# Reciprocal square roots and the causal mask's addition on VectorE in place of GpSimd, in a hybrid decoder block

## The chip, the cores and the metric

One of the cores of a Trainium2 chip runs the kernel. The core has five engines with an in-order queue each: TensorE (PE, with its weight loads shown apart as PEld), VectorE (DVE), ScalarE (ACT), GpSimd (POOL) and SyncE (SP), which here issues transfers. The metric is the device time of one execution in microseconds (us). Lower is better.

## The reference

The block works on 256 tokens of 2048 channels: a SwiGLU feed-forward of half weight, a token mixer, a second feed-forward, a gated per-layer embedding, and a last rmsnorm. The mixer has 8 gated delta-rule heads and 16 state-space heads in chunks that share one input and one output projection. Cut to what matters here:

```
def rmsnorm(x, w):
    return x * lax.rsqrt(jnp.mean(x * x, axis=-1, keepdims=True) + EPS) * w
def l2norm(x):
    return x * lax.rsqrt(jnp.sum(x * x, axis=-1, keepdims=True) + EPS)
...
    q = l2norm(q) * (GDN_HEAD_DIM ** -0.5)
    k = l2norm(k)
    ...
    decay = jnp.exp(jnp.where(causal, gc[..., :, None] - gc[..., None, :], -jnp.inf))
    ...
    t_inv = lax.linalg.triangular_solve(eye + lower, eye, left_side=True, lower=True)
    ...
    seg = jnp.exp(jnp.where(causal, acs[..., :, None] - acs[..., None, :], -jnp.inf))
    ...
    o = rmsnorm(o, norm_w) * jax.nn.silu(gate)
    ...
    proj = rmsnorm(h, mix_norm) @ w_in
    h = h + jnp.concatenate([o_gdn, o_ssm], axis=-1) @ w_out
```

## The kernel before

**The products.** Every weight matrix is streamed from HBM by SP (tile `raw`), a column tile of 128 columns at a time. Half a column tile (128x1024, 8 weight tiles of 128x128) is called a piece below: ACT rounds it to `hi` (L118), DVE makes the rest `lo` = `raw` - `hi` (L119), and PE multiplies both parts with the activations, 16 matmuls for each piece (`mm`, L128, L130, L132). ACT and DVE then bring the sum out of PSUM (L168, L169). There are 4 buffers each for `hi` and `lo` and 3 for `raw`. If DVE or ACT stands still, PE goes on with what is split already and then stands too.

**The token mixer.** It runs beside the product with `win` (52 column tiles, that is 104 pieces), as generators that `tick` advances by one step after each piece. For each of four pairs of delta-rule heads, `gdn_pair` builds the matrices `LA` (DVE, L533). SP writes their diagonal blocks to HBM (`blkl`) and reads them back in another layout (`Lb`). POOL inverts the blocks by substitution: 62 small instructions on `tb` and `Z` (L582, L584), a pair of them for each of 31 columns. SP takes the result back through HBM (`blky`, then four transfers into `Y`), and DVE transposes `Y` into `oT` (L595). Larger blocks, the chunk's state and the outputs `o` follow on PE, with DVE and ACT between (`xv` L642, `st` L635). Four `ssd_quad` generators do the state-space heads.

**What the change touches.** `rsq` (L207) is the reciprocal square root of a small tile. It is called 16 times: 8 times in `stats`, for the norms over channels, and 8 times in `gdn_pair`, for the lengths of keys and queries (`rs`, 128x8) and the norm of the outputs (`ro`, 128x4). `decay` (L490) is called 12 times, once for each pair and twice for each quad. A tile `dec` (128x512) is filled by a transfer that POOL issues (`spread`, L486), the causal mask is added to it (L492), ACT takes four exponentials of it (L494), and DVE multiplies it in `LA` (L533) or by `CB` (L747).

**The end of the projections.** The last columns of `win` give the gates `zt`. When the heads are done, ACT scales `o` by `ro` (L674), PE transposes it (`ot`, L679), ACT copies it to `oT` (L680), and DVE multiplies in the gate (L810). `osp` holds both parts of the mixer's output (`split_into`, L195 on ACT and L196 on DVE) and is what `wout` is multiplied with.

**The order.** A scheduler sorts the instructions of each engine when the program is built, by its own estimates of durations. On the chip each engine works through its list in that order, and an instruction that waits holds back all that stand behind it on its engine.

Of the kernel before, what the change touches and what calls it, by code (L numbers as in the profile page):

```python
# [10 lines left out]
F32R = mybir.dt.float32r  # L11
AF = mybir.ActivationFunctionType
# [3 lines left out]
P = 128  # L16
# [13 lines left out]
# columns of the parameter pack  # L30
# [12 lines left out]
# the inverse: diagonal blocks of BS, CG columns of one per partition, then doubled  # L43
# [4 lines left out]
# columns of the constant pack: identity, upper triangle, additive causal mask, level masks, unit columns  # L48
# [7 lines left out]
def constant_pack():  # L56
# [5 lines left out]
    # the columns of the identity that the partition holds, partition = (block, group of columns)  # L62
# [6 lines left out]
def tile_hybrid_block(ctx, tc, xT, pT, con, par, wgu1, wd1, wnar, win, wout, wgu2, wd2, wproj, wple, outT):  # L69
# [30 lines left out]
    # ---------------------------------------------------------------- helpers  # L100
# [6 lines left out]
    def load(src):  # L107
        """One transfer of the stationary tiles [P, n * 128] of one column tile."""
        raw = rawp.tile([P, 2048], F32, tag="raw", name="raw")
        nc.sync.dma_start(raw[:, :src.shape[-1]], src)  # L110
        return raw

    def split(src):
        """hi + lo = src exactly, each of them wide enough for one pass."""
# [7 lines left out]
    def chain(ps, hi, lo, act_in, ks, first=True, last=True):  # L122
        """ps[:, 0] (+)= (hi + lo) @ high part, ps[:, 1] (+)= hi @ low part of act_in, for the tiles w of
        hi + lo and the tiles k of act_in."""
# [10 lines left out]
    def single(src, act_in, ks):  # L135
        """The product as a whole in ps[:, 0]."""
# [14 lines left out]
    def product(srcs, act_in, ks, out):  # L151
        """out = the product of the column tile that lies in the transfers srcs, rows ks, with act_in."""
# [18 lines left out]
    # work that runs beside the products: each generator is advanced by one step after each piece  # L171
# [14 lines left out]
    def split_x(k, wname):  # L186
        """The parts of xs are those of h * w, for one k tile."""
# [5 lines left out]
    def split_into(dst, src):  # L193
        """dst[:, :, 0] + dst[:, :, 1] = src exactly."""
        act.copy(dst[:, :, 0, :], src)  # L195
        dve.tensor_tensor(out=dst[:, :, 1, :], in0=src, in1=dst[:, :, 0, :].bitcast(F32), op=ALU.subtract)  # L196

    def sumsq(acc, src, first):
        """acc[P, 2, T] += src^2, src a pair of tiles."""
# [7 lines left out]
    def rsq(m, n, name):  # L207
        """1/sqrt(m) for a [P, n] tile."""
        y = small.tile([P, n], F32, tag=f"rsq{n}", name=name)
        pool.tensor_tensor(out=y, in0=m, in1=mhalf[:, :n], op=ALU.pow)  # L210
        t = small.tile([P, n], F32, tag=f"rsqt{n}", name=name + "t")
        dve.tensor_tensor(out=t, in0=y, in1=y, op=ALU.mult)
        dve.scalar_tensor_tensor(out=t, in0=t, scalar=-0.5, in1=m, op0=ALU.mult, op1=ALU.mult)
        dve.scalar_tensor_tensor(out=y, in0=t, scalar=1.5, in1=y, op0=ALU.add, op1=ALU.mult)
        return y

    mhalf = cp.tile([P, 16], F32, name="mhalf")
    pool.memset(mhalf, -0.5)

    def stats(squares, width, name, use, wait=2):  # L220
        """use(row): 1/sqrt(mean over width channels + eps) per token, as a row on every partition (in PSUM).
        squares: [P, T] tiles whose sum over partitions and tiles is the sum of squares."""
# [29 lines left out]
    # ---------------------------------------------------------------- loads  # L252
    warm = small.tile([P, 1], F32, tag="warm", name="warm", bufs=1)
    act.activation(warm, ones[:, 0:1], AF.Silu)
    # the array's clock rises with use: multiply while the first transfers are on their way
# [5 lines left out]
    # the first transfers alternate between the tokens and the first three column tiles  # L261
# [28 lines left out]
    # ---------------------------------------------------------------- feed-forward  # L290
    def ffn(wgu, wd, squares, next_name, start=None):
        """h += 0.5 * swiglu(rmsnorm(h)); squares: gives those of h; returns those of the new h."""
# [50 lines left out]
    # ---------------------------------------------------------------- token mixer  # L343
    with ExitStack() as mix:
# [5 lines left out]
        # halved conv weights and bias: silu(2u) = u * (1 + tanh(u))  # L350
# [13 lines left out]
        # a pair of projected tiles, behind three columns of zeros  # L364
# [8 lines left out]
        # ---- per-token scalars: a (8), dt (16), b (8) -> decay logs, dt, beta  # L373
        raw = load(wnar)
        ps = mm_bank("nar")
        for k in range(0, KD, 8):
            # both parts as columns of one stationary tile: rows 0-31 and 32-63 of the product
# [30 lines left out]
        def scalars():  # L408
# [9 lines left out]
            # log(1 + e) = 2 atanh(e / (2 + e))  # L418
# [24 lines left out]
            # the cumulated logs as rows, in DRAM to be spread over the partitions from there  # L443
# [10 lines left out]
        # ---- projection of a pair of column tiles, causal conv, silu  # L454
# [18 lines left out]
        def silu_gate(w0):  # L473
            """Twice the silu."""
# [8 lines left out]
        def spread(src):  # L483
            """Rows of gc_i on every partition."""
# [5 lines left out]
        def decay(d, c):  # L490
            """exp(gc_i - gc_j) for j <= i, else 0, as [j, n, i]; d: rows of gc_i, c: columns of -gc_j."""
            pool.tensor_tensor(out=d, in0=d, in1=over(cmask, 4), op=ALU.add)  # L492
# [3 lines left out]
        # scratch for the diagonal blocks and their inverses  # L496
        blocks = [[tc.dram_tile([4 * (P // BS), BS, BS], F32, name=f"blk{n}{i}") for n in "ly"] for i in range(2)]

        # ---- gated delta rule, two heads at a time; matrices in the order (chunk, head)
        def gdn_pair(i, KQ, V):  # L500
# [12 lines left out]
            # squares of k (the diagonal of k k^T) and of q by token  # L513
# [36 lines left out]
            # diagonal blocks of I + L inverted by substitution, CG columns of one per partition  # L550
# [11 lines left out]
            # values and (first chunk) keys by token  # L562
# [375 lines left out]
def _rows(v):  # L938
    """[n * 128] -> [128, n]."""
    return v.reshape(-1, P).T  # L940
# [61 lines left out]
```

## Time and profile before

| | |
|---|---|
| device time, median of 3 runs | 2117.88 us (2116.24 to 2119.15) |
| span of the profiled execution, first to last instruction | 2115.8 us |
| PE busy | 2064.8 us, 98% of the span |
| DVE busy | 1351.4 us, 64% |
| ACT busy | 1047.7 us, 50% |
| POOL busy | 256.7 us, 12% |

The profiled execution has no time of its own beside its span; the runs' median is 2.1 us above that span. The first feed-forward ends near 760 us of the span, the projections of the mixer near 1162 us, and the rest is the output projection, the second feed-forward, the embedding and the last norm. POOL's share is an average over a program in which it does little outside the mixer. In a list of waits the engine on the left stood idle until the engine on the right ended the instruction that is named.

### The profile page before, as it was taken

Reading aid. Unit: us, or ns where it says so; the run is one execution under the profiler, and the core shown is the slowest. Engines: PE = TensorE matmul, PEld = TensorE weight load, DVE = VectorE, ACT = ScalarE, POOL = GpSimd, SP = SyncE. Lnnn points to the kernel's source line nnn. Section 1 sums busy time; section 2 is a strip of 40 time slices with the busy share of each in tenths; the row PEclk is TensorE's granted clock in tenths of the full one; section 3 lists DMA queues with packets and bytes.
Section 4 is the critical chain, followed back from the end, with each engine's and each line's share of the span. In section 5 each row is a group of like instructions: output and inputs, shape, how many; then the busy total and the mean of one; then the engine's idle time right before and its main releaser. Section 6 shows DMA issues by size and latency. Waiting matters only on the chain.

```text
span 2115.8 us, 29521 instructions
## 1 busy us (share of the span) xinstructions
PE 2064.8 (98%) x11824; PEld 1795.9 (85%) x11824; DVE 1351.4 (64%) x1908; ACT 1047.7 (50%) x1591; POOL 256.7 (12%) x368
## 2 busy tenths in 40 slices
PE   9999999999999999888989999999999999999997
PEld 7888888888888888777878888888888888888886
DVE  7655555656556677767777666665555556556685
ACT  6444444444445555444455556544444444445554
POOL 2000000000000011667540011000000000000011
PEclk9999999999999999998999999999999999999998
DMA  7555455555545555434544555555456555545652
GB/s 261 187 182 195 158 190 184 207 191 188 182 172 179 190 198 164 163 123 148 168 137 151 194 179 187 191 189 190 163 183 211 185 193 180 190 160 190 201 194 101
DMA packets 67129, 380.77 MB, mean 180 GB/s; under 512 B 11744, under 2 KB 13024, under 8 KB 33840
## 3 DMA queue, kind: packets, MB, share of 16 engines
q1 hardware_dynamic: 65664, 374.93, 52.3%
q0 software_dynamic: 1328, 3.97, 1.0%
q8 instruction: 92, 1.51, 0.3%
q14 instruction: 45, 0.37, 0.1%
HBM read 376.21 MB, written 2.65 MB: 179 GB/s over the span
## 4 chain that ended last, share of the span: by engine, by line
PE 85%; POOL 7%; DMA 3%; issue 2%; DVE 2%; SPq 0%; ACT 0%; POOLq 0%; DVEq 0%; ACTq 0%
PE mm L130 55%; PE mm L128 26%; POOL Z L584 3%; POOL tb L582 3%; PE mm L132 2%; DMA Lb<-blkl 1%; DMA blkl<-LA 1%; DMA er<-rows 1%; DVE lo L119 1%; DMA Y<-blky 0%; PE pj L130 0%; DMA hT<-in_xT 0%; DVE LA L533 0%; POOL dec L486 0%; POOL dec L492 0%
## 5 line engine op out<-in xcount | busy, mean ns | idle before, releaser
L130 PE MATMUL mm<-xs,hi 128*128 128x512 f32 x3888 | 1367.0, 399 | 1.8 <-ACT hi L118 1.8
L119 DVE TENSOR_TENSOR lo<-raw,hi 128x1024 fp32r<-128x1024 f32 (+1 forms) x774 | 864.2, 1124 | 489.8 <-ACT hi L118 489.4
L128 PE MATMUL mm<-xs,lo 128*128 128x256 f32 x3645 | 1028.8, 282 | 6.4 <-DVE lo L119 6.4
L118 ACT CAST hi<-raw 128x1024 fp32r<-128x1024 f32 (+1 forms) x774 | 745.7, 964 | 517.7 <-PE mm L130 403.5
L130 PEld LDWEIGHTS mm<-xs,hi 128*128 128x128 f32 x3888 | 718.5, 189 | 155.9 <-ACT hi L118 2.3
L128 PEld LDWEIGHTS mm<-xs,lo 128*128 128x128 f32 x3645 | 687.5, 189 | 20.8 <-DVE lo L119 8.4
L130 PE MATMUL mm<-hid,hi 128*128 128x512 f32 x1408 | 492.5, 397 | 0.0
L128 PE MATMUL mm<-hid,lo 128*128 128x256 f32 x1344 | 377.8, 281 | 0.0
L130 PEld LDWEIGHTS mm<-hid,hi 128*128 128x128 f32 x1408 | 260.2, 188 | 59.0
L205 POOL TENSOR_TENSOR acc<-acc,sq 128x512 f32<-128x512 f32 x43 | 65.6, 1525 | 1602.3 <-ACT sq L204 1578.0
L128 PEld LDWEIGHTS mm<-hid,lo 128*128 128x128 f32 x1344 | 253.3, 188 | 3.0
L168 ACT COPY t<-mm 128x256 f32<-128x256 f32 x167 | 62.4, 374 | 158.5 <-PE mm L130 157.6
L169 DVE TENSOR_TENSOR t<-t,mm 128x256 f32<-128x256 f32 x167 | 69.9, 419 | 85.7 <-ACT t L168 85.4
L168 ACT COPY s<-mm 128x256 f32<-128x256 f32 x88 | 32.8, 373 | 148.2 <-PE mm L130 148.1
L130 PE MATMUL mm<-osp,hi 128*128 128x512 f32 x256 | 88.9, 396 | 0.0
L169 DVE TENSOR_TENSOR s<-s,mm 128x256 f32<-128x256 f32 x88 | 37.1, 421 | 73.7 <-ACT s L168 73.6
L132 PE MATMUL mm<-xs,lo 128*128 128x256 f32 x243 | 69.6, 286 | 11.7 <-DVE lo L119 11.7
L584 POOL TENSOR_TENSOR Z<-Z,tb 128x124 f32<-128x124 f32 (+30 forms) x124 | 67.8, 547 | 9.4
L128 PE MATMUL mm<-osp,lo 128*128 128x256 f32 x240 | 67.1, 281 | 0.0
L132 PEld LDWEIGHTS mm<-xs,lo 128*128 128x128 f32 x243 | 45.9, 189 | 24.5 <-DVE lo L119 14.1
L582 POOL TENSOR_TENSOR tb<-Lb,Z 128x124 f32<-128x124 f32 (+30 forms) x124 | 61.7, 498 | 27.0 <-DMA Lb<-blkl 17.9
L130 PEld LDWEIGHTS mm<-osp,hi 128*128 128x128 f32 x256 | 46.9, 188 | 10.1
(296 smaller groups left out, 1091.4 us busy)
## 6 DMA issues: line engine op xcount, KB each, us to landing
raw<-in_wgu SPq DMA_DIRECT2D x173, 1024.0 KB, 4.8
raw<-in_wd SPq DMA_DIRECT2D x128, 704.0 KB, 4.1
raw<-in_win SPq DMA_DIRECT2D x52, 1024.0 KB, 5.0
raw<-in_wout SPq DMA_DIRECT2D x16, 1024.0 KB, 4.9
raw<-in_wple SPq DMA_DIRECT2D x16, 1024.0 KB, 4.8
first<-in_wgu SPq DMA_DIRECT2D x12, 256.0 KB, 7.2
dec<-rows POOLq DMA_DIRECT2D x12, 256.0 KB, 4.7
Lb<-blkl SPq DMA_DIRECT2D x4, 512.0 KB, 5.2
```

Of the source, the lines that this page charges most:

```text
L118: act.copy(hi, src)
L119: dve.tensor_tensor(out=lo, in0=src, in1=hi.bitcast(F32), op=ALU.subtract)
L128: pe.matmul(ps[:, 0, :], lo[:, w, :], act_in[:, k, 0, :], start=False, stop=False, skip_group_check=True)
L130: pe.matmul(ps, hi[:, w, :], act_in[:, k], start=start, stop=stop, skip_group_check=True)
L132: pe.matmul(ps[:, 0, :], lo[:, w, :], act_in[:, k, 0, :], start=False, stop=False, skip_group_check=True)
L168: act.copy(out, ps[:, 0, :])
L169: dve.tensor_tensor(out=out, in0=out, in1=ps[:, 1, :], op=ALU.add)
L205: pool.tensor_tensor(out=acc, in0=acc, in1=sq, op=ALU.add)
L582: pool.tensor_tensor(out=t, in0=over(Lb[:, j, j + 1:], CG), in1=Z[:, :, j:j + 1].to_broadcast([P, CG, n]), op=ALU.mult)
L584: pool.tensor_tensor(out=Z[:, :, j + 1:], in0=Z[:, :, j + 1:], in1=t, op=ALU.subtract)
```

## The change

`rsq` no longer calls `pow` on POOL. DVE makes a first guess from the bits of the number (a shift, then a multiplication and an addition) and improves it by three Newton steps of three instructions, where one step of three followed `pow` before. The tile `mhalf` and its memset go. In `decay` the addition of the mask moves from POOL to DVE. All else in the diff is comments and docstrings.

```
+I32 = mybir.dt.int32
...
     def rsq(m, n, name):
         """1/sqrt(m) for a [P, n] tile."""
         y = small.tile([P, n], F32, tag=f"rsq{n}", name=name)
-        pool.tensor_tensor(out=y, in0=m, in1=mhalf[:, :n], op=ALU.pow)
         t = small.tile([P, n], F32, tag=f"rsqt{n}", name=name + "t")
-        dve.tensor_tensor(out=t, in0=y, in1=y, op=ALU.mult)
-        dve.scalar_tensor_tensor(out=t, in0=t, scalar=-0.5, in1=m, op0=ALU.mult, op1=ALU.mult)
-        dve.scalar_tensor_tensor(out=y, in0=t, scalar=1.5, in1=y, op0=ALU.add, op1=ALU.mult)
+        dve.tensor_scalar(t.bitcast(I32), m.bitcast(I32), 1, None, op0=ALU.logical_shift_right)
+        dve.tensor_scalar(y.bitcast(I32), t.bitcast(I32), -1.0, float(0x5F3759DF), op0=ALU.mult, op1=ALU.add)
+        for _ in range(3):
+            dve.tensor_tensor(out=t, in0=y, in1=y, op=ALU.mult)
+            dve.scalar_tensor_tensor(out=t, in0=t, scalar=-0.5, in1=m, op0=ALU.mult, op1=ALU.mult)
+            dve.scalar_tensor_tensor(out=y, in0=t, scalar=1.5, in1=y, op0=ALU.add, op1=ALU.mult)
         return y
-    mhalf = cp.tile([P, 16], F32, name="mhalf")
-    pool.memset(mhalf, -0.5)
...
         def decay(d, c):
-            pool.tensor_tensor(out=d, in0=d, in1=over(cmask, 4), op=ALU.add)
+            dve.tensor_tensor(out=d, in0=d, in1=over(cmask, 4), op=ALU.add)
```

The scheduler sorts the changed program anew. In what follows most helper lines of the changed program stand one line further down than before (L120 for L119, L131 for L130, L169 for L168, L197 for L196); the lines of `rsq` are L212, L213 (the guess) and L215 to L217 (a Newton step), and lines from L232 on have the same numbers.

On POOL, in the substitution of pair 2 (the third), the program before has this in the middle of the 62 steps, between the columns of 60 and of 48: the transfers of two `dec` tiles (those of pair 3 and of the first half of quad 1), their two additions, and two transfers for `er`.

```order
L582 TENSOR_TENSOR tb<-Lb,Z 128x60
L486 DMA dec<-rows 128x2x256
L486 DMA dec<-rows 128x512
L584 TENSOR_TENSOR Z<-Z,tb 128x4x15
L582 TENSOR_TENSOR tb<-Lb,Z 128x56
L584 TENSOR_TENSOR Z<-Z,tb 128x4x14
L492 TENSOR_TENSOR dec<-dec,cont 128x512
L582 TENSOR_TENSOR tb<-Lb,Z 128x52
L727 DMA er<-rows 64x2x128 x2
L492 TENSOR_TENSOR dec<-dec,cont 128x512
L584 TENSOR_TENSOR Z<-Z,tb 128x4x13
```

In the changed program the same transfers stand behind the last step of that substitution:

```order
L582 TENSOR_TENSOR tb<-Lb,Z 128x4
L584 TENSOR_TENSOR Z<-Z,tb 128x4
L486 DMA dec<-rows 128x2x256
L486 DMA dec<-rows 128x512
L560 COPY Z<-cont 128x128
L727 DMA er<-rows 64x2x128 x2
L590 MEMSET Y 128x512
L486 DMA dec<-rows 128x512
L582 TENSOR_TENSOR tb<-Lb,Z 128x124
```

So the two `dec` tiles are asked for some 30 steps later, and their additions, now on DVE, stand in DVE's list three pieces further on than the place at which DVE waited for them before. In pair 3 the transfers that stood in the middle (for quad 2) move likewise, to two or three steps before its end.

On PE, at the end of the projections, the program before transposes the outputs of the last pair (`ot`) among the last pieces of the product with `win` (`mm<-xs`), 66 matmuls ahead of its end:

```order
L130 MATMUL mm<-xs,hi 128x512
L679 MATMUL ot<-cont,o 128x128
L128 MATMUL mm<-xs,lo 128x256
L679 MATMUL ot<-cont,o 128x128
L130 MATMUL mm<-xs,hi 128x512
L679 MATMUL ot<-cont,o 128x128 x2
L130 MATMUL mm<-xs,hi 128x512
L132 MATMUL mm<-xs,lo 128x256
```

In the changed program they stand behind the last matmul of that product, right ahead of the first one of the output projection (`mm<-osp`):

```order
L129 MATMUL mm<-xs,lo 128x256
L131 MATMUL mm<-xs,hi 128x512
L679 MATMUL ot<-cont,o 128x128 x4
L131 MATMUL mm<-osp,hi 128x512
L133 MATMUL mm<-osp,lo 128x256
L129 MATMUL mm<-osp,lo 128x256
```

No matmul of a product is left there between what makes `o` and what needs it. On DVE the rows of the changed program at this place are these, from the last gate `zt` (L170, which needs the end of the product with `win`) on; `rot` and `ro` are the reciprocal square root of the last pair's outputs:

```order
L170 TENSOR_TENSOR zt<-zt,mm 128x256
L217 SCALAR_TENSOR_TENSOR ro<-rot,ro 128x4
L478 TENSOR_TENSOR zt<-zt,r 128x512
L215 TENSOR_TENSOR rot<-ro 128x4
L120 TENSOR_TENSOR lo<-raw,hi 128x1024
L480 SCALAR_TENSOR_TENSOR zt<-zth,zt 128x512
L217 SCALAR_TENSOR_TENSOR ro<-rot,ro 128x4
L672 TENSOR_TENSOR ro<-ro,rq 128x4
L810 SCALAR_TENSOR_TENSOR oT<-oT,hgn,zt 128x512
L197 TENSOR_TENSOR osp<-yT,osp 128x2x256 x4
L197 TENSOR_TENSOR osp<-oT,osp 128x2x256 x4
L197 TENSOR_TENSOR psp<-praw,psp 128x2x256
```

The end of that square root now stands behind the last gate, and the eight rows of `osp` behind it; before, `ro` of the last pair stood seven pieces ahead of the last gate (L478), and six of the eight `osp` rows four pieces ahead of it.

## Rows read from the trace of the kernel before

**Rows 1.** The page, part 1: busy us (share of the span) and instructions of each engine.

```profile
PE 2064.8 (98%) x11824; PEld 1795.9 (85%) x11824; DVE 1351.4 (64%) x1908; ACT 1047.7 (50%) x1591; POOL 256.7 (12%) x368
```

**Rows 2.** Windows: length, then busy us (instructions) by engine, clock, DMA share, GB/s.

```profile
984.00:1000.00 16.00, 7.49 (x33) 6.46 (x32) 7.10 (x12) 7.44 (x17) 11.84 (x24) 0.68 0.30 59
1150.00:1180.00 30.00, 30.00 (x173) 26.08 (x173) 23.23 (x32) 18.52 (x28) 0.61 (x1) 1.00 0.51 172
```

**Rows 3.** PE's waits: what it waited for, us in total, times, longest us.

```profile
PE st L635 <- DVE xv L642: 16.2, 2, 8.5
PE mm L132 <- DVE lo L119: 11.7, 4, 9.3
```

**Rows 4.** Timeline of DVE, start of pair 1: start, us, instruction [idle before <-releaser].

```profile
880.81 0.17 DVE L212 TENSOR_TENSOR rst<-rs 128x8 f32<-128x8 f32 x1 [10.68 <-POOL rs L210]
...
882.60 1.22 DVE L119 TENSOR_TENSOR lo<-raw,hi 128x1024 fp32r<-128x1024 f32 x1
...
886.03 0.71 DVE L595 STREAM_TRANSPOSE oT<-Y 128x512 f32<-128x512 f32 x1
```

**Rows 5.** Timeline of SP's queue there.

```profile
880.74 1.75 SPq L592 DMA_DIRECT2D Y<-blky  x4
882.58 1.89 SPq L554 DMA_DIRECT2D blkl<-LA  x4
```

**Rows 6.** Timeline of POOL: the substitutions of pairs 0 to 3.

```profile
845.44 0.40 POOL L582 TENSOR_TENSOR tb<-Lb,Z 128x124 f32<-128x124 f32 x1 [3.83 <-DMA Lb<-blkl]
...
870.18 0.29 POOL L582 TENSOR_TENSOR tb<-Lb,Z 128x56 f32<-128x56 f32 x1
...
878.96 0.20 POOL L584 TENSOR_TENSOR Z<-Z,tb 128x4 f32<-128x4 f32 x1
...
894.00 1.21 POOL L582 TENSOR_TENSOR tb<-Lb,Z 128x124 f32<-128x124 f32 x1 [6.06 <-DMA Lb<-blkl]
...
933.78 0.20 POOL L584 TENSOR_TENSOR Z<-Z,tb 128x4 f32<-128x4 f32 x1
...
983.03 1.33 POOL L486 DMA_DIRECT2D dec<-rows  x2 [0.18 <-issue]
...
988.30 1.26 POOL L492 TENSOR_TENSOR dec<-dec,cont 128x512 f32<-128x512 f32 x1 [2.87 <-DMA dec<-rows]
...
1030.46 1.85 POOL L582 TENSOR_TENSOR tb<-Lb,Z 128x124 f32<-128x124 f32 x1 [3.23 <-DMA Lb<-blkl]
```

**Rows 7.** Timeline of DVE, pairs 2 and 3.

```profile
991.85 1.53 DVE L119 TENSOR_TENSOR lo<-raw,hi 128x1024 fp32r<-128x1024 f32 x1 [13.18 <-ACT hi L118]
...
1001.52 1.24 DVE L119 TENSOR_TENSOR lo<-raw,hi 128x1024 fp32r<-128x1024 f32 x1
...
1019.28 1.66 DVE L533 SCALAR_TENSOR_TENSOR LA<-kk,c,dec 128x256 f32<-128x256 f32 x4
...
1091.27 1.22 DVE L119 TENSOR_TENSOR lo<-raw,hi 128x1024 fp32r<-128x1024 f32 x1
```

**Rows 8.** Timeline of ACT at the end of the projections.

```profile
1146.32 1.29 ACT L674 ACTIVATE o<-o,ro 128x128 f32<-128x128 f32 x4
...
1150.96 0.37 ACT L168 COPY zt<-mm 128x256 f32<-128x256 f32 x1 [2.00 <-PE mm L130]
...
1152.18 0.59 ACT L680 COPY oT<-ot 128x512 f32<-128x512 f32 x1
```

**Rows 9.** Timeline of DVE there.

```profile
1151.82 0.69 DVE L478 TENSOR_TENSOR zt<-zt,r 128x512 f32<-128x512 f32 x1
...
1153.57 2.49 DVE L196 TENSOR_TENSOR osp<-yT,osp 128x512 fp32r<-128x512 f32 x4
...
1158.91 0.75 DVE L810 SCALAR_TENSOR_TENSOR oT<-oT,hgn,zt 128x512 f32<-128x512 f32 x1
```

**Rows 10.** Timeline of DVE, the last norm.

```profile
2105.29 0.16 DVE L212 TENSOR_TENSOR finalt<-final 128x2 f32<-128x2 f32 x1 [0.82 <-POOL final L210]
2105.48 0.16 DVE L213 SCALAR_TENSOR_TENSOR finalt<-finalt,finalm 128x2 f32<-128x2 f32 x1
```

## The prediction, made before the changed kernel ran

> **What bounds the kernel now.** I read the page's busy times first. PE is busy for 2064.8 of 2115.8 us [rows 1], so the kernel is bound by PE nearly everywhere, and a change to DVE and POOL can win at most the some 51 us in which PE stands. DVE is 64% busy on average, so it has room outside the mixer. Then I read what PE waits for. Two kinds of wait hold most of it: 16.2 us in two pieces on `xv`, and 9.3 us in one piece on `lo` [rows 3]. All three lie in the mixer. The timelines tell what stands behind each of them, and all three lead to POOL.
>
> The 9.3 us: DVE waits 10.68 us for `pow` of pair 1's `rs` [rows 4]. `pow` stands in POOL's list behind the whole substitution of pair 0, which ends at 879.2 [rows 6]. DVE's next `lo` comes at 882.60, and PE starves until then.
>
> The 8.5 us, and the like in pair 3 (16.2 - 8.5 = 7.7): DVE waits 13.18 us for `hi` [rows 7], because ACT's exponentials stand ahead of that `hi` and need POOL's addition of the mask. POOL asked for that tile in the middle of its substitution at 983.03 and adds at 988.30 [rows 6].
>
> A long stall costs more than its idle time: between 984 and 1000 us the granted clock is 0.68, so part of it runs at the lower of the two levels. At the rate of a full stretch, 173 matmuls in 30 us or 5.77 per us [rows 2], 16 us hold 92 matmuls; 33 were done, so 10.2 us are lost, of which 8.5 are the stall. That leaves 1.7 us for the clock.
>
> **The change, part by part.** The sum is made on the profiled execution's span of 2115.8 us; I add what it gives to the runs' median of 2117.88, which lies 2.1 us above.
>
> *Pair 1's start.* `pow` goes, so DVE passes that place and builds `LA` of pair 1 at once. But in the changed order the next thing there that can wait is the transpose of pair 0's `Y` into `oT`, one piece earlier than before. It needs the end of the same substitution, and then the trip through HBM: `Y` is asked for at 880.74 [rows 5] and was there by 886.03, when the transpose ran without a wait [rows 4]. With 4 to 5 us for the transfer DVE's next `lo` comes near 886 rather than 882.60, some 3 us later. The stall moves and grows. What follows is not late, though. `blkl` of pair 1 stands in SP's list behind those transfers of `Y` (882.58, rows of the same list [rows 5]), whether or not `LA` is ready, so the substitution of pair 1 starts at 894.00 as now. It ends near 934 [rows 6] and its result sets the next wait. The 3 us are given back there. Together: 0.
>
> *Pair 2.* POOL no longer adds in the middle, nor asks for `dec` there. That frees it from 983.03 on. From that step to the end pair 0 needed 9.0 us (870.18 to 879.16), while DVE stood; beside a working DVE it goes slower: the whole substitution took 33.7 us in pair 0, of which the end was undisturbed, and 39.8 in pair 1 [rows 6]. I take 995 for the end. Only then are the two `dec` tiles asked for. From asking to adding took 5.27 us (983.03 to 988.30), so DVE's additions run near 1001, and the `lo` behind them comes near 1002.5. DVE now meets this wait three pieces later, and the `lo` at that place ran at 1001.52 before [rows 7]. So PE is 1 us later than now, with the clock's 1.7 us still to pay: about 2 late. The stall is not removed, because the transfer and not the addition is what is late.
>
> *Pair 3.* `LA` of pair 3 stands four pieces further on than before (1019.28). Four pieces with what lies between took 12 to 15 us there (16 pieces from 1019.28 to 1091.27 are 4.5 us each with two stalls in them), so `LA` comes near 1033, and after the 11.2 us that it took before (1019.28 to 1030.46) the substitution begins near 1044 [rows 6, 7]. With 37 us, between the two cases above, it ends at 1081. The tiles of quad 2 are asked for two or three steps before that end and land 5.3 us later, at 1085.5. Then come two additions of 0.69 (the price of a 128x512 product of two operands on DVE, [rows 9]), exponentials and two multiplications, and the `lo` behind them near 1089.5 against 1091.27 before. At this point the changed kernel is 1.8 us ahead, less the clock's share: the whole chain through the four pairs gives **-1.5 us**. Its bounds come from the lengths of the substitutions: 33.7 us for both would give -8, and 45 (the price beside DVE's added work of 128 small instructions and 12 additions) +8.
>
> *The end of the projections.* This is new. Before, `o` of the last pair was scaled at 1146.32, copied to `oT` at 1152.18 [rows 8], and PE was busy for all of 1150 to 1180 [rows 2]. In the changed order all of this stands behind the last gate `zt`, so it begins when PE has ended its last matmul with `win`, and nothing but `ot` stands in PE's list ahead of the output projection. Step by step: from ACT's copy of `zt` to the multiplication with `r` 0.86 us (1150.96 to 1151.82); that multiplication 0.69; a small step of the square root 0.15 and a `lo` of 1.22; the gate's product, of the same shape, 0.69; two more small ones 0.4 [rows 4, 8, 9, 10]. That makes 4.0. ACT's four scalings take 1.29, PE's last transpose about 0.3 (an estimate, from matmuls of 0.17 us each in rows 2), ACT's copy 0.59, DVE's gate 0.75, the first `osp` 0.62 (2.49 over four). That is 7.55 us in which PE does nothing of a product. The pieces of the output projection are split already by then (four buffers), and its `osp` rows of 0.62 for two tiles keep ahead of PE, which needs 0.7 for 4 matmuls. With 1.7 us for the clock: **+9.2 us**. Lower bound 5.0, if the clock stays up and the links overlap by a third; upper 13, if the second half's `osp` holds PE as well.
>
> *The norms.* In the last norm nothing hides the square root. Before it cost 0.82 for POOL and three dependent steps, 0.19 apart (2105.29, 2105.48) [rows 10]; now it is eleven such steps, 2.1 us against 0.82 + 0.57. **+0.7 us.** The seven other calls in `stats` lie beside products that PE has in store, and DVE's idle third covers eight steps of 0.19; uncovered they would cost 0.7 each, 5 us in all, which I keep for the upper end. The shift and the guess on integers are in no row; I price them like the small DVE rows, 0.19 from one to the next [rows 10]; between nothing and twice that, the sum moves by 0.4 at most. The memset of `mhalf` ran in the first us and is worth nothing.
>
> Sum: -1.5 + 9.2 + 0.7 = +8.4, so **2126 us**.
>
> **A rule of the Trainium skill.** The Trainium skill (GPSIMD Engine Reference, 1. Specifications) says that GpSimd shares its way to SBUF with VectorE and that the two contend when a DVE instruction has two inputs in SBUF; the moved addition has two. By that rule each addition holds POOL from DVE's side instead, for 0.69 us, and the substitutions are longer beside a busier DVE. The trace agrees so far: 33.7 us with DVE idle at the end, 39.8 with DVE at work [rows 6].
>
> **The rivals.**
>
> 1. *Faster: the waits vanish.* If `Y` and `dec` land before DVE reaches them, all three stalls go: 9.3 + 16.2 + 3 x 1.7 = 30.6 us, less 9.9 for the end and the norm: about 2097; with half of them gone 2112. For it: all three waits are for POOL, and the work in its way moves off. Against: the changed order puts the same or later transfers behind the same substitutions. It is decided by whether `Y` and the `dec` tiles have landed when DVE comes to them. 0.2.
>
> 2. *No change: the end of the projections is filled.* If the `ot` chain costs nothing, -1.5 + 0.7 gives 2117. For it: PE was never idle there. Against: the order leaves PE nothing else. This holds likewise if the chain gives back 8 us and the end costs 9. 0.2.
>
> 3. *Slower by more: the substitutions grow.* DVE's 12 additions and 128 more small instructions, at 0.69 and 0.08 to 0.19 us (18 to 33 us in all), run mostly beside the four substitutions. If two of those on the path take 45 us rather than 37, the chain is +8 and each wait on `dec` grows to some 15 to 20 us: 2136 to 2140. The rule of the Trainium skill above (GPSIMD Engine Reference, 1. Specifications) speaks for this one. 0.15.
>
> **How the numbers follow.** My forecast, 2120 to 2133 for itself, has 0.45. No change means within 0.2% or 4.2 us, about what a measurement of this kernel can tell. The forecast's low edge lies in it, the others as said: faster 0.2, same 0.2, slower 0.6. The range goes from 2110 (half of the first rival) to 2139 (the third).
>
> **What would show it.** Right: no `pow` and no addition on POOL; DVE waits for `Y` in pair 0 and for `dec` tiles in pairs 2 and 3, the latter behind the last steps of the substitution; PE stands for 7 to 8 us between the last `mm<-xs` and the first `mm<-osp`, then runs at the lower clock; eleven DVE steps ahead of `finalrow`. Wrong: PE busy through the end of the projections, waits on `lo` and `xv` of under 3 us, or a DVE so full in the mixer that PE waits for `lo` at many places by a little.

## The result, and the profile after

The changed kernel takes 2131.45 us (2130.93 to 2131.9, 4 runs) against 2118.52 us before (2116.24 to 2120.94, 4 runs). The ratio is 1.0058, with a 95% interval of 1.0044 to 1.0072. The change makes the kernel slower by 0.6%, 12.9 us. The forecast was 2126, in a range of 2110 to 2139. The span of the profiled execution is 2129.1 us, 13.3 more than before.

The page's first part, of the changed kernel:

```profile
PE 2065.0 (97%) x11824; PEld 1796.0 (84%) x11824; DVE 1368.8 (64%) x2048; ACT 1045.6 (49%) x1591; POOL 217.2 (10%) x339
```

PE does the same 11824 matmuls as before and is busy for as long [rows 1]: 2065.0 against 2064.8 us. By this page all that was added is time in which PE stands; the windows further down show that a part of the loss is a lower clock, too. POOL lost 39.5 us of work and DVE gained 17.4; neither figure says anything of the time.

What PE waited for (us in total, times, longest):

```profile
PE ip L606 <- DVE oT L595: 16.7, 1, 16.7
PE st L635 <- DVE xv L642: 11.0, 1, 11.0
PE ss L751 <- DVE xe L744: 7.2, 1, 7.2
PE ot L679 <- ACT o L674: 4.2, 1, 4.2
...
PE mm L131 <- DVE osp L197: 2.1, 1, 2.1
...
PE finalrow L238 <- DVE final L217: 2.4, 1, 2.4
```

The three stalls of the mixer are still there [rows 3]: 16.7 us (before 9.3), 11.0 (before 8.5) and 7.2 (before 7.7). New are `ot` and `osp`, at the end of the projections, and `finalrow` has grown from 1.6 us (the same view of the kernel before) to 2.4.

How much each part of the program costs is read by three marks that both kernels have: ACT's last copy of a gate (`zt`), which follows PE's last matmul with `win`; its 16th and last copy of the output projection (`wo`); and the first and last steps of the last norm. The timeline of ACT before (start, us, instruction, idle before it and its releaser):

```profile
1162.47 0.38 ACT L168 COPY zt<-mm 128x256 f32<-128x256 f32 x1 [0.94 <-PE mm L130]
...
1252.60 0.37 ACT L168 COPY wo<-mm 128x256 f32<-128x256 f32 x1 [1.74 <-PE mm L130]
```

The same of the changed kernel, with the scaling of `o` and the copy of `oT` between the two marks:

```profile
1164.30 0.37 ACT L169 COPY zt<-mm 128x256 f32<-128x256 f32 x1 [1.72 <-PE mm L131]
...
1168.04 1.28 ACT L674 ACTIVATE o<-o,ro 128x128 f32<-128x128 f32 x4 [1.52 <-DVE ro L672]
1169.89 0.59 ACT L680 COPY oT<-ot 128x512 f32<-128x512 f32 x1 [0.57 <-PE ot L679]
...
1265.15 0.37 ACT L169 COPY wo<-mm 128x256 f32<-128x256 f32 x1 [1.73 <-PE mm L131]
```

From the start to the last `zt` the changed kernel loses 1.83 us (1162.47 to 1164.30). From there to the last `wo` it takes 100.85 us against 90.13: 10.72 more. The last norm on DVE, from `finalm` to the first product with `finalrow`, before:

```profile
2104.08 0.38 DVE L232 TENSOR_SCALAR finalm<-final 128x1 f32<-128x1 f32 x2 [0.92 <-PE final L229]
...
2107.15 4.87 DVE L912 TENSOR_TENSOR pp<-pp,finalrow 128x256 f32<-128x256 f32 x8 [1.31 <-PE finalrow L238]
```

The same in the changed kernel, with the first two and the last of its eleven steps:

```profile
2116.54 0.39 DVE L232 TENSOR_SCALAR finalm<-final 128x1 f32<-128x1 f32 x2 [0.92 <-PE final L229]
2116.97 0.17 DVE L212 TENSOR_SCALAR finalt<-finalm 128x2 int32<-128x2 int32 x1
2117.17 0.17 DVE L213 TENSOR_SCALAR final<-finalt 128x2 int32<-128x2 int32 x1
...
2118.94 0.16 DVE L217 SCALAR_TENSOR_TENSOR final<-finalt,final 128x2 f32<-128x2 f32 x1
2120.41 4.87 DVE L912 TENSOR_TENSOR pp<-pp,finalrow 128x256 f32<-128x256 f32 x8 [1.31 <-PE finalrow L238]
```

It takes 3.87 us against 3.07: 0.80 more. What lies between the last `wo` and `finalm` is the second feed-forward and the embedding; it takes 851.39 us against 851.48, so the square roots of the norms there cost nothing. Nor do those ahead of the mixer's pairs: up to 830 us of the span PE does 4675 matmuls in the changed kernel and 4669 before. Together 1.83 + 10.72 + 0.80 - 0.09 = 13.26 us, which is the difference of the spans.

The end of the projections in the changed kernel, on DVE:

```profile
1164.71 0.42 DVE L170 TENSOR_TENSOR zt<-zt,mm 128x256 f32<-128x256 f32 x1 [0.20 <-ACT zt L169]
...
1165.16 0.69 DVE L478 TENSOR_TENSOR zt<-zt,r 128x512 f32<-128x512 f32 x1
...
1165.84 1.22 DVE L120 TENSOR_TENSOR lo<-raw,hi 128x1024 fp32r<-128x1024 f32 x1
...
1167.05 0.68 DVE L480 SCALAR_TENSOR_TENSOR zt<-zth,zt 128x512 f32<-128x512 f32 x1
...
1167.84 0.16 DVE L672 TENSOR_TENSOR ro<-ro,rq 128x4 f32<-128x4 f32 x1
1170.51 0.75 DVE L810 SCALAR_TENSOR_TENSOR oT<-oT,hgn,zt 128x512 f32<-128x512 f32 x1 [2.50 <-ACT oT L680]
1171.18 2.49 DVE L197 TENSOR_TENSOR osp<-yT,osp 128x512 fp32r<-128x512 f32 x4
```

The rows stand as the order had it. The last gate's sum begins at 1164.71, the product with `r` at 1165.16, a `lo` at 1165.84, the gate's product at 1167.05, and only then is `ro` ready (1167.84). ACT scales `o` at 1168.04, copies `oT` at 1169.89, DVE brings in the gate at 1170.51 and makes the first `osp` at 1171.18. Before, ACT scaled the last `o` 16 us ahead of its last `zt` [rows 8]. What PE waits for last, 2.1 us long, is `osp` made of `yT`, the state-space half of the mixer's output. DVE's last step on `yT` began at 1158.6, so this half was complete 12 us before `osp` was made of it: it needs nothing of the last pair, and stood in DVE's list behind that pair's gate. The windows there, of the changed kernel (length; busy us and instructions of PE, PEld, DVE, ACT, POOL; clock; DMA share; GB/s):

```profile
1164.00:1168.50 4.50, 0.27 (x3) 0.01 (x1) 3.70 (x12) 2.41 (x5) 0.00 (x0) 0.91 0.53 166
1168.50:1172.00 3.50, 1.44 (x5) 0.81 (x5) 1.49 (x3) 2.93 (x8) 0.00 (x0) 0.50 0.63 262
1172.00:1182.00 10.00, 10.00 (x42) 8.67 (x43) 5.52 (x9) 4.20 (x8) 0.57 (x1) 0.70 0.10 28
```

PE stands, then does the four transposes, stands again, and runs at a clock of 0.70 for the ten us that follow: 42 matmuls, where the full rate of 5.77 per us [rows 2] gives 58. So of the 10.72 us 6.3 are idle (4.2 + 2.1), 1.4 are the transposes, which now have PE to themselves (1168.49 to 1169.85), and 2.7 are the clock; 0.3 is left over.

### The profile page after: what moved, and what is told of

The parts are those of the page before. It is cut to its first block, busy times and chain, and to the rows that moved or that the text cites. A ratio compares the mean times of both kernels' runs of the same rounds, so it can differ in the third digit from the quotient of the medians.

```text
span 2129.1 us, 29626 instructions
## 1 busy us (share of the span) xinstructions
PE 2065.0 (97%) x11824; PEld 1796.0 (84%) x11824; DVE 1368.8 (64%) x2048; ACT 1045.6 (49%) x1591; POOL 217.2 (10%) x339
## 4 chain that ended last, share of the span: by engine, by line
PE 48%; POOL 1%; DVE 1%; DMA 1%; issue 0%; ACT 0%; SPq 0%; DVEq 0%; POOLq 0%
PE mm L131 31%; PE mm L129 15%; PE mm L133 1%; POOL Z L584 1%; POOL tb L582 1%; PE pj L131 0%; DMA Lb<-blkl 0%; DMA dec<-rows 0%; DVE pp L912 0%; DMA blkl<-LA 0%; PE py L759 0%; DVE u L467 0%; DVE lo L120 0%; PE o L635 0%; PE mm L148 0%
## 5 line engine op out<-in xcount | busy, mean ns | idle before, releaser
L131 PE MATMUL mm<-xs,hi 128*128 128x512 f32 x3888 | 1363.1, 399 | 2.6 <-DVE zt L170 1.7
L120 DVE TENSOR_TENSOR lo<-raw,hi 128x1024 fp32r<-128x1024 f32 (+1 forms) x774 | 862.2, 1121 | 474.6 <-ACT hi L119 473.8
L119 ACT CAST hi<-raw 128x1024 fp32r<-128x1024 f32 (+1 forms) x774 | 743.5, 961 | 519.0 <-PE mm L131 418.5
L131 PEld LDWEIGHTS mm<-xs,hi 128*128 128x128 f32 x3888 | 717.6, 189 | 158.1 <-DVE zt L170 1.9
L131 PE MATMUL mm<-hid,hi 128*128 128x512 f32 x1408 | 492.5, 397 | 0.0
L131 PEld LDWEIGHTS mm<-hid,hi 128*128 128x128 f32 x1408 | 260.2, 188 | 59.1
L169 ACT COPY t<-mm 128x256 f32<-128x256 f32 x167 | 62.1, 373 | 158.5 <-PE mm L131 157.5
L170 DVE TENSOR_TENSOR t<-t,mm 128x256 f32<-128x256 f32 x167 | 69.8, 418 | 85.1 <-ACT t L169 85.0
L169 ACT COPY s<-mm 128x256 f32<-128x256 f32 x88 | 32.8, 372 | 149.8 <-PE mm L131 149.8
L131 PE MATMUL mm<-osp,hi 128*128 128x512 f32 x256 | 91.6, 405 | 2.1 <-DVE osp L197 2.1
L170 DVE TENSOR_TENSOR s<-s,mm 128x256 f32<-128x256 f32 x88 | 37.0, 421 | 74.3 <-ACT s L169 74.3
L582 POOL TENSOR_TENSOR tb<-Lb,Z 128x124 f32<-128x124 f32 (+30 forms) x124 | 66.3, 535 | 50.0 <-DMA Lb<-blkl 40.6
L131 PEld LDWEIGHTS mm<-osp,hi 128*128 128x128 f32 x256 | 48.3, 193 | 13.0 <-DVE osp L197 2.4
L584 POOL TENSOR_TENSOR Z<-Z,tb 128x124 f32<-128x124 f32 (+30 forms) x124 | 56.8, 458 | 9.7
```

What stands on the lines that cost most here:

```text
L119: act.copy(hi, src)
L120: dve.tensor_tensor(out=lo, in0=src, in1=hi.bitcast(F32), op=ALU.subtract)
L131: pe.matmul(ps, hi[:, w, :], act_in[:, k], start=start, stop=stop, skip_group_check=True)
L169: act.copy(out, ps[:, 0, :])
L170: dve.tensor_tensor(out=out, in0=out, in1=ps[:, 1, :], op=ALU.add)
L582: pool.tensor_tensor(out=t, in0=over(Lb[:, j, j + 1:], CG), in1=Z[:, :, j:j + 1].to_broadcast([P, CG, n]), op=ALU.mult)
```

## The experiments

My theory, after the result: the loss is an order. The square root of each pair's outputs (`ro`) has become so long on DVE that the scheduler puts the last pair's transposes behind the last matmul with `win`, and PE then has nothing to do. A rival is that the 12 additions of the mask cost the time on DVE; another that DVE is simply fuller, by 128 small instructions.

**One half of the change at a time.** `rsq_only` puts the addition back on POOL:

```
-            dve.tensor_tensor(out=d, in0=d, in1=over(cmask, 4), op=ALU.add)
+            pool.tensor_tensor(out=d, in0=d, in1=over(cmask, 4), op=ALU.add)
```

> All 16 square roots on VectorE, the mask's addition back on GpSimd. First theory (the longer square root of the last pair's outputs sets the order at the end of the projections): the transposes of the outputs still stand behind the last matmul of the projections, so that stretch still costs 10 to 11 us and the last norm 0.8; with the chain of the four pairs at -3 to +5 the time is 2127 to 2136 us. Second theory (the 12 additions on VectorE are the cost): no more than 2120 us. Third theory (VectorE is simply fuller): most of the added instructions are here, 2125 to 2132 us, with the loss spread over many short waits for lo.

Measured: 2133.64 us, 1.0074 (1.0059 to 1.0089). All of the loss is there. In the profiled execution the last `zt` comes 3.1 us later than in the changed kernel (table below), but that execution took 1.5 us longer than this kernel's median, and the two kernels' intervals overlap, so it is not shown that this one is slower still. The time is also 1.6 us above what the third theory allowed.

`mask_only` is the kernel before with that line the other way round.

> The 12 additions of the mask on VectorE, the square roots as before (pow on GpSimd, one Newton step). First theory: the end of the projections is as before the change, and the tiles with the decay are asked for 12 to 16 steps earlier in pair 2 than before, so its stall shrinks from 8.5 us to under 4: 2108 to 2118 us. Second theory: the loss comes with the additions, 2126 us or more. Third theory: 2119 to 2121 us, some 8 us of additions with most of it hidden.

Measured: 2117.88 us, 1.0002 (0.9992 to 1.0012). Moving the addition is free. It falls within the first theory's time, but brings nothing of the gain that its low end stood for: PE's stall of 8.5 us for `xv` is gone, but PE now stands 7.5 us for `Y` (L611) there, where under 4 us were expected. The second theory falls with these two runs.

**One of the square roots alone.** `all_but_ro` is the changed kernel with the four calls on `ro` back at `pow` and one step:

```
+        if name in ('ro',):
+            pool.tensor_tensor(out=y, in0=m, in1=mhalf[:, :n], op=ALU.pow)
+            dve.tensor_tensor(out=t, in0=y, in1=y, op=ALU.mult)
+            dve.scalar_tensor_tensor(out=t, in0=t, scalar=-0.5, in1=m, op0=ALU.mult, op1=ALU.mult)
+            dve.scalar_tensor_tensor(out=y, in0=t, scalar=1.5, in1=y, op0=ALU.add, op1=ALU.mult)
+            return y
...
+    mhalf = cp.tile([P, 16], F32, name="mhalf")
+    pool.memset(mhalf, -0.5)
```

> The changed kernel with one thing undone: the square root of the outputs of each pair (128x4, four calls) is again pow on GpSimd and one Newton step. First theory: the transposes of the outputs stand ahead of the end of the projections again and PE is idle there for less than 1 us, so 10 to 11 us come back, and the tiles with the decay are asked for in the middle of the third substitution again: 2112 to 2121 us. Second and third theory: 96 of the 128 added small instructions and all 12 additions are still there, so at least three quarters of the loss stays: 2128 us or more.

Measured: 2115.68 us, 0.9991 (0.9981 to 1.0000). `only_ro` is the reverse: the kernel before with only these four calls on DVE. (One clause of the text on record is a slip: the changed kernel has the mask's addition on VectorE. In `only_ro` it is on GpSimd, as before the change.)

> The kernel before with one thing done: the square root of the outputs of each pair (128x4, four calls) on VectorE; the other 12 square roots are pow, and as in the changed kernel the mask's addition is not on VectorE but here stays on GpSimd. First theory: these four calls alone put the transposes behind the last matmul of the projections, which costs 10 to 11 us; the last norm costs nothing, and the chain of the pairs -3 to +5: 2126 to 2134 us. Second theory: 2118 us, as before. Third theory: a quarter of the added instructions, so 2119 to 2121 us.

Measured: 2128.38 us, 1.0047 (1.0032 to 1.0062). Four calls of 16, 32 rows of 128, bring most of the loss by themselves (1.0047 against 1.0058), and without them none is left. The third theory, by which the loss should go with the number of instructions, falls. The window from 1160 to 1185 us of `all_but_ro` (columns as in the windows above):

```profile
1160.00:1185.00 25.00, 25.00 (x143) 21.75 (x143) 18.82 (x26) 14.96 (x23) 0.61 (x1) 1.00 0.54 185
```

The same of `only_ro`:

```profile
1160.00:1185.00 25.00, 18.70 (x91) 15.53 (x90) 16.45 (x32) 13.48 (x25) 0.59 (x1) 0.80 0.33 113
```

PE is busy throughout in the one and runs at full clock; in the other it stands for 6.3 us here and runs at 0.80.

**Engine or length.** `ro` may cost this because it left POOL, or because it is long. `ro_one_step` and `ro_two_steps` keep it on DVE and shorten it (the second has a 2 in place of the 1):

```
-        for _ in range(3):
+        for _ in range(1 if name == "ro" else 3):
```

> The changed kernel with one Newton step in place of three in the square root of the outputs of each pair (128x4, four calls), which leaves that result less exact; nothing goes back to GpSimd. First theory, now in the form that the length of this one square root on VectorE decides where the scheduler puts the transposes of the last pair's outputs: in this build they stand 42 matmuls ahead of the end of the projections, so the 10 to 11 us of that stretch come back: 2113 to 2121 us. Rival: it is the engine that counts and not the length (the four calls on VectorE cost what they cost because pow beside it was free): 24 rows of 128 fewer, 2127 to 2131 us.

> The same with two Newton steps in these four calls. In this build the transposes stand behind the last matmul of the projections again, but the scaling of the outputs stands ahead of the last gate's tanh on ScalarE, so the way from the end of the projections to the first part of the mixer's output is some 2 us shorter. First theory: most of the loss of that stretch is back, 2123 to 2130 us, a jump of 7 us or more against one step. Rival: twelve rows more than with one step at 0.2 us each, at most 2.4 us more than with one step.

Measured: 2118.04 us, 0.9999 (0.9989 to 1.0008) with one step, and 2125.63 us, 1.0038 (1.0024 to 1.0052) with two. The jump of 7.6 us comes with three instructions in each of four calls, 12 rows of 0.2 us. The same window with one step:

```profile
1160.00:1185.00 25.00, 25.00 (x145) 21.83 (x144) 19.14 (x26) 14.26 (x21) 0.58 (x1) 1.00 0.65 220
```

and with two:

```profile
1160.00:1185.00 25.00, 21.06 (x107) 17.52 (x106) 18.32 (x31) 15.74 (x28) 0.57 (x1) 0.86 0.45 141
```

It is the length, by way of the order: with one step the transposes stand 42 matmuls ahead of the end of `win`, with two behind it. The marks of these kernels, from the same three views (us):

| kernel | last `zt` | `zt` to 16th `wo` | last norm |
|---|---|---|---|
| before | 1162.47 | 90.13 | 3.07 |
| changed | 1164.30 | 100.85 | 3.87 |
| `rsq_only` | 1167.41 | 102.07 | 3.86 |
| `mask_only` | 1161.61 | 90.13 | 2.98 |
| `all_but_ro` | 1161.74 | 89.67 | 3.86 |
| `only_ro` | 1162.12 | 100.23 | 3.27 |
| `ro_one_step` | 1161.18 | 90.03 | 3.86 |
| `ro_two_steps` | 1162.18 | 97.52 | 3.86 |

The middle column takes 90 us where the transposes stand ahead of the end of `win` and 97.5 to 102 us where they stand behind it. Within the second group it goes with how long the transposes wait for ACT's scaling of `o`: 1.7 us with two steps, 4.2 in `only_ro` and the changed kernel, 6.7 in `rsq_only`. No kernel here moves the transposes with the square roots left as they are; that the order is the way is read from this column and from PE's waits. The first one stays between 1161 and 1168 us whatever was moved.

**The last norm.** `all_but_ro_final` gives `pow` back to the last norm too (`if name in ('ro', 'final')`).

> The changed kernel with pow on GpSimd for the square root of the outputs of each pair and for that of the last norm. The last norm's eleven dependent steps cost 0.8 us more than pow and one step, so this should be 0.8 us faster than the kernel in which only the outputs' square root was undone: 2114 to 2116 us. A rival (the embedding's own square roots, which are still on VectorE near the end, cover or add to it): no difference.

Measured: 2115.5 us, 0.9991 (0.9982 to 1.0000). The trace has the 0.8 us (3.07 as before, against 3.86), but the times, 2115.5 and 2115.68, do not tell the two kernels apart. It is inconclusive as a timing.

**The waits in pairs 2 and 3.** I had put these down to the transfers of `dec`, which stand amid POOL's substitutions. In `all_but_ro_dec_sp` SP issues them, where the order puts them ahead of the substitution's end:

```
-            nc.gpsimd.dma_start(d.rearrange("p (c n) i -> p c n i", c=src.shape[0]),
+            nc.sync.dma_start(d.rearrange("p (c n) i -> p c n i", c=src.shape[0]),
```

> The changed kernel with pow on GpSimd for the square root of each pair's outputs, and with the transfers of the decay tiles issued by SyncE in place of GpSimd. First theory (what is late in pairs 2 and 3 is the transfer that waits in GpSimd's list amid the substitution, and not the addition): VectorE's waits for these tiles (8.1, 6.6 and 4.8 us with GpSimd) fall under 2 us, PE gains 4 to 10 us of which the waits for Y take some back: 2106 to 2114 us. Rival: SyncE's list holds them back behind its own waits for Y and for free buffers of the weights, or the weights' stream comes late: 2115 us or more.

Measured: 2117.71 us, 1.0007 (0.9997 to 1.0016). No gain. The waits of 8.1 and 6.6 us for `dec` are gone and the third one stays (4.7 us), but ACT now waits for the next transfer that POOL issues there, `er` (ACT's waits in 950 to 1000 us; in 1050 to 1100 us it is 10.9):

```profile
ACT er L743 <- DMA er<-rows: 12.2, 1, 12.2
```

So in three more kernels SP issues both `dec` and `er`: `all_but_ro_final`, `mask_only` and the kernel before, each with these two edits and nothing else. The second edit is the same on the line of `er`:

```
-                nc.gpsimd.dma_start(er[64 * hh:64 * hh + 64],
+                nc.sync.dma_start(er[64 * hh:64 * hh + 64],
```

> The changed kernel with pow on GpSimd for the square root of each pair's outputs and of the last norm, and with both kinds of small transfers of the mixer (the decay tiles and er) issued by SyncE. With the decay tiles alone on SyncE, VectorE's wait for them in pair 2 was gone but ScalarE waited 12.2 and 10.9 us for er, which GpSimd still asked for amid the substitution. First theory (the transfers in GpSimd's list are what is late): both waits go and PE's waits on xv and S in pairs 2 and 3 fall from some 15 us to under 6: 2104 to 2111 us. Rival (the pairs' chain is set by the substitutions and their trip through HBM, and a wait removed comes back as a longer one at the next Y): 2113 to 2117 us.

> The mask's addition on VectorE, all square roots as before, and the decay tiles and er issued by SyncE. First theory: the additions no longer wait for a tile, GpSimd's substitutions are not interrupted: 2105 to 2112 us. Rival as for the kernel beside it: 2114 to 2119 us.

> The kernel before with nothing but the decay tiles and er issued by SyncE; the additions stay on GpSimd, amid the substitutions. First theory: the wait for the tile goes but the addition still stands in GpSimd's list, which is on time when the tile is: 2107 to 2115 us. Rival: 2115 to 2119 us. If this gains as much as the kernel beside it with the additions on VectorE, moving the additions was worth nothing by itself.

Measured: 2118.64 us, 1.0002 (0.9993 to 1.0010); 2123.19 us, 1.0022 (1.0013 to 1.0030); 2119.96 us, 1.0009 (1.0000 to 1.0018). None of the three gains, as the rival said, and all three come out above its range, the second by 4 us. Where the gain goes is seen in `all_but_ro_final_sp`, on DVE: pair 3's addition, the transpose of pair 2's `Y`, and the first addition of the last quad:

```profile
983.87 1.49 DVE L501 TENSOR_TENSOR dec<-dec,cont 128x512 f32<-128x512 f32 x2
...
1018.70 0.71 DVE L604 STREAM_TRANSPOSE oT<-Y 128x512 f32<-128x512 f32 x1 [14.21 <-DMA Y<-blky]
...
1080.23 0.69 DVE L501 TENSOR_TENSOR dec<-dec,cont 128x512 f32<-128x512 f32 x1 [10.65 <-DMA dec<-rows]
```

The transfers for that last addition stand in SP's list behind the one that takes the last substitution's result to HBM (`blky`), as they stood behind the last step of that substitution in POOL's list:

```profile
1073.90 0.33 SPq L594 DMA_DIRECT2D blky<-Z  x1
...
1074.80 0.84 SPq L495 DMA_DIRECT2D dec<-rows  x2
```

The windows of this kernel:

```profile
960.00:1010.00 50.00, 49.79 (x325) 43.90 (x324) 41.54 (x79) 29.38 (x59) 35.03 (x62) 1.00 0.42 133
1010.00:1060.00 50.00, 41.59 (x250) 34.92 (x250) 39.14 (x97) 23.80 (x55) 22.14 (x37) 0.93 0.58 182
1060.00:1110.00 50.00, 40.71 (x255) 35.43 (x254) 34.83 (x69) 24.19 (x52) 15.53 (x32) 0.90 0.45 140
```

The same windows of `all_but_ro` (the last norm, in which the two differ besides, comes some 950 us later):

```profile
960.00:1010.00 50.00, 43.03 (x266) 37.42 (x265) 39.21 (x73) 24.95 (x52) 34.73 (x68) 0.93 0.51 168
1010.00:1060.00 50.00, 45.58 (x295) 40.15 (x293) 40.50 (x96) 26.76 (x59) 27.36 (x53) 0.99 0.45 140
1060.00:1110.00 50.00, 48.34 (x304) 42.51 (x305) 40.46 (x82) 25.70 (x53) 16.86 (x24) 0.94 0.50 164
```

From 960 to 1010 us PE gains 6.8 us (49.79 against 43.03), because the addition at 983.87 waits for nothing. From 1010 to 1060 it gives back 4.0 (41.59 against 45.58): DVE reaches `Y` earlier and waits 14.21 us for it. From 1060 to 1110 it gives back 7.6 more (40.71 against 48.34): DVE waits 10.65 us for the last quad's tile, 4.75 in `all_but_ro`, and PE 9.3 us for an `xv` that stands behind that addition. The last `zt` of this kernel's profiled execution comes at 1168.73, against 1160.84 in the kernel without the two moves. That difference of 7.9 us is too large as a measure of the two kernels: the execution was the longest of its eleven, 2124.07 us, and the medians are 3.1 us apart.

I read this as a pace that the four substitutions set, one behind the other with a trip through HBM between them: a wait taken away ahead of one of them is waited for again behind it. That is not shown, and the traces speak against it as the whole account. In the changed kernel the substitutions of pairs 2 and 3 are 10.6 and 13.0 us shorter than before (34.4 and 33.7 against 961.26 to 1006.28 and 1030.46 to 1077.11 on POOL before, 45.0 and 46.7), and the last one still ends 1.7 us later (1078.8 against 1077.1). In `only_ro` the last one ends 7.8 us earlier than before (1069.3), and the last `zt` comes only 0.35 us earlier. So a shorter substitution alone brings nothing either, and what sets the time of this stretch stays open. The prediction was right that the transfers of `dec` are what DVE waits for there. What its first rival would be worth, with every tile there in time, is not settled, since the last quad's tiles were still asked for behind the end of a substitution. `mask_only_sp` has the longest such wait (13.6 us for that tile, PE 10.6 us for an `xv`); whether it makes all of the 5 us that this kernel lost against `mask_only` is not shown.

## Why the prediction was right, point by point

The forecast was slower, by 8.4 us, and the measured 12.9 us lies inside its range. The main mechanism was named, and shown by experiment: the end of the projections, which the order of the changed program alone told. Counted on the spans, the sum fell 4.9 us short (13.3 against 8.4): 1.5 at the end of the projections and 3.3 in the chain of the pairs, and nothing in the norms together.

**The end of the projections** was put at +9.2 and measured at +10.7. The way through the engines is as worked out: 7.55 us were forecast, and PE did nothing of a product for 4.2 + 1.4 + 2.1 = 7.7. The term that was too small is the clock, 1.7 us from the stall at 984, against 2.7 here: the clock was 0.50 while the transposes ran and 0.70 for the ten us behind them. That the order is due to `ro` was not in the prediction; the experiments added it.

**The chain of the four pairs** was put at -1.5, between -8 and +8, and came out at +1.8 at the last `zt`. The timeline of DVE in the changed kernel:

```profile
887.67 0.71 DVE L595 STREAM_TRANSPOSE oT<-Y 128x512 f32<-128x512 f32 x1 [14.90 <-DMA Y<-blky]
...
1003.82 1.48 DVE L492 TENSOR_TENSOR dec<-dec,cont 128x512 f32<-128x512 f32 x2 [13.96 <-DMA dec<-rows]
...
1005.55 1.22 DVE L120 TENSOR_TENSOR lo<-raw,hi 128x1024 fp32r<-128x1024 f32 x1
...
1031.55 1.65 DVE L533 SCALAR_TENSOR_TENSOR LA<-kk,c,dec 128x256 f32<-128x256 f32 x4
...
1079.39 0.69 DVE L492 TENSOR_TENSOR dec<-dec,cont 128x512 f32<-128x512 f32 x1 [9.46 <-DMA dec<-rows]
...
1085.25 1.22 DVE L120 TENSOR_TENSOR lo<-raw,hi 128x1024 fp32r<-128x1024 f32 x1
```

and that of POOL:

```profile
893.23 0.39 POOL L582 TENSOR_TENSOR tb<-Lb,Z 128x124 f32<-128x124 f32 x1 [9.93 <-DMA Lb<-blkl]
...
998.19 0.20 POOL L584 TENSOR_TENSOR Z<-Z,tb 128x4 f32<-128x4 f32 x1
998.69 1.30 POOL L486 DMA_DIRECT2D dec<-rows  x2 [0.30 <-issue]
...
1045.11 0.43 POOL L582 TENSOR_TENSOR tb<-Lb,Z 128x124 f32<-128x124 f32 x1 [10.79 <-DMA Lb<-blkl]
...
1075.12 1.12 POOL L486 DMA_DIRECT2D dec<-rows  x2 [0.29 <-issue]
...
1078.58 0.21 POOL L584 TENSOR_TENSOR Z<-Z,tb 128x4 f32<-128x4 f32 x1
```

*Pair 1's start*: the wait moved from `pow` to `Y`, as forecast, and the substitution of pair 1 starts at 893.23 (forecast 894.00). The stall grew by 7.4 us and not by 3, as PE itself waited for `oT` (`ip`). Most of it was given back at the next `Y`, as forecast, but not all: from 830 to 960 us PE did 641 matmuls against 656, that is 2.6 us at the full rate, and the substitution of pair 2 began at 963.96 against 961.26 before. The 0 of this term should have been some 2.7. *Pair 2*: the substitution took 34.4 us, where the forecast's end at 995 stands for 33.7, so the end came at 998.39. The additions were forecast near 1001 and ran at 1003.82; the `lo` behind them near 1002.5, and it ran at 1005.55. The transfer asked for at 998.69, behind the last step, is what DVE waited 13.96 us for. *Pair 3*: `LA` was forecast near 1033 and ran at 1031.55, the substitution from 1044 to 1081 and ran from 1045.11 to 1078.78. The tiles came six us earlier than forecast (1079.39 against 1085.5), and the `lo` behind them ran at 1085.25, 6.0 us ahead of before [rows 7]. That lead was gone at the end of `win`. Two windows of the changed kernel:

```profile
1080.00:1110.00 30.00, 27.65 (x173) 23.57 (x174) 29.37 (x59) 20.38 (x49) 6.03 (x7) 0.90 0.38 115
1100.00:1164.00 64.00, 64.00 (x408) 56.57 (x408) 52.18 (x116) 30.90 (x59) 2.19 (x2) 1.00 0.46 155
```

From 1080 to 1110 us DVE is busy for 29.37 of 30 us, with the pair's and the quads' work that stood behind the additions. PE stood for 2.35 us there, all of it ahead of that `lo`. From 1100 to 1164 PE was never idle and did 408 matmuls, 6.4 per us, against 382 in the 62 us to the end of `win` before, 6.2 per us: small matmuls of the last pair and quads that had been done earlier came there. Counted from the two `lo` on, with 24 pieces still to split in both kernels, PE did 504 matmuls in 79.0 us up to the end of `win`, against 441 in 71.2 us before; 54 of the 63 more are such small ones. So the lead was DVE's and not PE's. The step that was mis-sized is that one: I counted the chain as over when the last tiles of the decay had come, with the work behind them still ahead.

The bounds of this term do not follow from its own numbers. The sum has 33.7 us for pair 2's substitution (961.26 to 995) and 37 for pair 3's, so 33.7 for both gives -4.8 and not -8, and 45 for both +18 and not +8; the third rival has the same +8. The low end of the range, 2110, is called half of the first rival, which the rival's own sum puts at 2112.

**The last norm** was put at +0.7 and measured at +0.8. The eleven steps run from 2116.97, 0.2 apart. **The other norms** were put at nothing: 851.39 against 851.48 us.

**The rivals.** The waits did not vanish, and the end of the projections was not filled. The substitutions did not grow either: with DVE waiting for a part of them those of pairs 2 and 3 took 34.4 us (963.96 to 998.39) and 33.7, where before, with the additions and transfers amid them, they took 45.0 and 46.7. That of pair 1 beside a busy DVE took 40.1. The Trainium skill (GPSIMD Engine Reference, 1. Specifications) has GpSimd and VectorE contend for their shared way to SBUF when a DVE instruction has two inputs there. These lengths agree with it, but no run separates it from other causes. Moving the additions onto DVE cost nothing that can be measured (`mask_only`, 1.0002).

## What to carry to other kernels

Where a scheduler sorts the queues, a longer chain of small instructions costs what its last consumer's place costs: twelve rows of 0.2 us moved four transposes behind the last matmul of a product, and that was worth 7.6 us. So read the new order at the seams between products, where nothing else is left for TensorE, before pricing the moved instructions. And where stages run in series through GpSimd and HBM, judge the removal of a wait by a mark behind the last stage and not by the stretch in which it stood: here a wait of 8.1 us removed ahead of one stage won PE 6.8 us there, and PE lost 11.6 us in the 100 us behind it.

## What the runs showed of the hardware that was not expected

The first ten us after the stall at the end of the projections ran at a granted clock of 0.70 and lost 2.7 us, where the window around the stall of 8.5 us at 984 lost 1.7. Integer shifts and multiplications on 128x2 take 0.17 us on VectorE, like the float steps at 0.16, and in a chain all of them are 0.2 us apart, so eleven cost 2.1 us.
